# K and Q of head 0 in float32, ahead of the norm, for both halves of the sequence, with an opening in a fixed order

## The chip, the cores and the metric

The kernel runs on one core of a Trainium2 chip. The core has TensorE for matrix products (PE in the profile; PEld is its loading of weights), VectorE (DVE), ScalarE (ACT), GpSimd (POOL) and SyncE (SP, whose queue issues the DMAs here). The metric is the device time of one execution in microseconds (us); less is better.

## The reference

Two layers of a decoder with x of 1024 positions by 1024 channels, float32. What matters here is the start of layer 0: the norm, the projections, and the differential attention.

```python
u = rmsnorm(h, attn_norm[l])
proj = u @ w_in[l]
rq, rk, rv, rg, dq, dk, dv = jnp.split(proj, offsets, axis=-1)
...
dif = diff_attention(dq.reshape(B, S, DIFF_HEADS, 2, DIFF_HEAD_DIM),
                     dk.reshape(B, S, DIFF_HEADS, 2, DIFF_HEAD_DIM),
                     dv.reshape(B, S, DIFF_HEADS, DIFF_V_DIM), lam)
...
s = jnp.einsum('bqhjd,bkhjd->bhjqk', qb, kb).astype(jnp.float32) * scale
p = jax.nn.softmax(s, axis=-1)
a = p[:, :, 0] - lam * p[:, :, 1]
```

`rmsnorm` divides each position by the root of its mean square and multiplies by a gain per channel. Each of four heads has two score maps j of 64 channels, swept in blocks of 128 queries. Retention, the output projection, SwiGLU and layer 1 follow and are not touched.

## The kernel before

Everything is held with channels on the partitions and positions along the free dimension; the 1024 positions are two halves of 512 (`NH`, `HT`), the 1024 channels eight tiles (`KT`). Precision comes from splitting: a float32 value becomes a high part in float32r (a cast on ScalarE) and a low part, the remainder (a subtraction, on GpSimd for weights and on VectorE for u), and a product is three float32r matmuls, high by high, high by low and low by high (`mm3`, lines 288 to 290 in the profile; lines 323 to 325 are the same three in `tm_pair`, which makes the values V in pairs of position tiles, 256 columns each).

The opening of layer 0 runs in this order. x's half 0 and the weights of K and Q of head 0 are loaded in pieces. `fm_first` multiplies the unnormed x by weights into which the gains have been folded, in true float32 matmuls (line 307; one such matmul leaves two records in the trace), while the norm of half 0 is still being found: squares on ScalarE, their sums over channel tiles on VectorE (line 433), the sum over partitions by matmuls with ones (line 398), the root, and transposes that spread it over the partitions (line 414). `norm_half` then makes u in eight steps: a multiply (line 446), a cast (448) and a low part (450). K and Q of half 0 come by multiplying the product in PSUM by the root (line 696) and are put into stacks of high and low parts by `stack` (lines 522 and 523). Half 1 has the same norm, woven into the values of half 0; its K and Q are made from u with the split weights.

Then head 0's blocks: `att_block` makes the scores of both maps (lines 574 and 575), takes bias and maximum on VectorE (line 577), the exponential on ScalarE (581), scales and subtracts the maps (657, 666), and one block later `att_turn` transposes the result (line 600) for the product with V. `weave` puts other matmuls between: it takes from a fill so that the share of the fill that is done keeps up with that of the blocks. A unit of both is about one matmul of 512 columns. In head 0 the fill of blocks 0 to 3 is K, Q and V of half 1 (96 units), that of blocks 4 to 7 is K and Q of head 1 (96 units).

TensorE's order is the order in which the program is written, and each engine works off its own list in order. Outside `feed_forward`, the lists of the other engines and of SP's queue are set by a scheduler, which lets stacks and a few other operations go ahead (`high_priority`).

## Time and profile before

| | us |
|---|---|
| three runs: median (lowest to highest) | 2291.11 (2290.65 to 2291.35) |
| the profiled execution's own time | 2289.39 |
| its span, from the first to the last instruction | 2287.6 |
| TensorE busy in it | 2251.1 (98%) |
| VectorE busy | 1404.7 (61%) |
| ScalarE busy | 1009.1 (44%) |
| GpSimd busy | 731.7 (32%) |

The span is read against TensorE's busy time first: the difference is the time in which TensorE has nothing to do. "Busy" for a matmul includes its way through the array, so in a dense stream the distance from one start to the next is the cost of one and not its duration. In a row, the brackets at the end give the idle time of the engine just before it and what ended that.

### The profile page before, as it was taken

The numbers are of one execution on the slowest core, as the hardware profiler recorded it, in microseconds if no ns is written. First come the engines' busy times: TensorE is split into PE (matmuls) and PEld (weight loads), VectorE is DVE, ScalarE is ACT, GpSimd is POOL, SyncE is SP. The second block draws the span as 40 slices with busy tenths as digits, with TensorE's granted clock in tenths as the row PEclk, the third lists the DMA queues.
The fourth block names the chain that finished last, engine by engine and source line by source line (L and its number), as shares of the span: only waits on it lengthen the run. The fifth ranks groups of instructions, "written<-read, shape, count | busy, mean of one in ns | idle before, by whom it ended". The sixth has DMA issues, their size and how long they took to land.

```text
span 2287.6 us, 30632 instructions
## 1 busy us (share of the span) xinstructions
PE 2251.1 (98%) x11328; PEld 1895.3 (83%) x11328; DVE 1404.7 (61%) x2596; ACT 1009.1 (44%) x1905; POOL 731.7 (32%) x588
## 2 busy tenths in 40 slices
PE   7999999999999999999999999999999999999998
PEld 5888898787888888888888888988878888888887
DVE  8777612989534333995567774059884434359856
ACT  5666523445333333543256665234453333344332
POOL 3111212120455555335121112211215445544350
PEclk9999999999999999999999999999999999999999
DMA  4212121112433333652232222112123232346422
GB/s 164 79 47 65 44 95 38 55 57 63 137 106 103 105 106 90 230 186 96 72 99 56 56 65 88 52 37 74 49 95 120 93 115 93 110 148 202 157 65 74
DMA packets 74215, 216.58 MB, mean 95 GB/s; under 512 B 8017, under 2 KB 10065, under 8 KB 74065
## 3 DMA queue, kind: packets, MB, share of 16 engines
q1 hardware_dynamic: 74064, 214.62, 29.1%
q8 instruction: 89, 1.46, 0.3%
q14 instruction: 62, 0.50, 0.1%
HBM read 162.16 MB, written 44.04 MB: 90 GB/s over the span
## 4 chain that ended last, share of the span: by engine, by line
PE 84%; DVE 11%; ACT 2%; issue 1%; DMA 1%; POOL 0%; SPq 0%; DVEq 0%; ACTq 0%; POOLq 0%
PE ps_mm L264 8%; PE ps_mm L265 8%; PE ps_mm L266 8%; PE ps_mm L289 7%; PE ps_mm L288 7%; PE ps_mm L290 7%; PE ps_s L265 4%; PE ps_s L264 4%; PE ps_s L266 4%; PE ps_mm L323 3%; PE ps_mm L324 3%; PE ps_mm L325 3%; PE ps_t L265 2%; PE ps_t L264 2%; PE ps_t L266 2%
## 5 line engine op out<-in xcount | busy, mean ns | idle before, releaser
L241 POOL TENSOR_TENSOR w<-wr,w 128x512 fp32r<-128x512 f32 x262 | 368.2, 1419 | 442.9 <-ACT w L240 425.6
L281 POOL TENSOR_TENSOR w<-wr,w 128x512 fp32r<-128x512 f32 x140 | 186.2, 1337 | 577.3 <-ACT w L280 520.7
L288 PE MATMUL ps_mm<-u,w 128*128 128x512 f32 (+1 forms) x735 | 296.1, 403 | 0.0
L289 PE MATMUL ps_mm<-u,w 128*128 128x512 f32 (+1 forms) x735 | 287.2, 391 | 2.4 <-DVE u L450 2.4
L290 PE MATMUL ps_mm<-u,w 128*128 128x512 f32 (+1 forms) x735 | 286.5, 390 | 0.0
L240 ACT CAST w<-wr 128x512 fp32r<-128x512 f32 x312 | 187.2, 619 | 136.5 <-DVE wr L911 77.5
L264 PE MATMUL ps_mm<-u,w 128*128 128x512 f32 x432 | 168.5, 390 | 0.0
L266 PE MATMUL ps_mm<-u,w 128*128 128x512 f32 x432 | 168.1, 389 | 0.0
L265 PE MATMUL ps_mm<-u,w 128*128 128x512 f32 x432 | 168.1, 389 | 0.0
L290 PEld LDWEIGHTS ps_mm<-u,w 128*128 128x128 f32 x735 | 138.1, 188 | 30.1
L289 PEld LDWEIGHTS ps_mm<-u,w 128*128 128x128 f32 x735 | 138.6, 189 | 26.0 <-DVE u L450 3.1
L288 PEld LDWEIGHTS ps_mm<-u,w 128*128 128x128 f32 x735 | 138.3, 188 | 23.7
L960 ACT COPY t<-ps_mm 128x512 f32<-128x512 f32 x76 | 44.7, 588 | 240.3 <-PE ps_mm L266 240.3
L280 ACT CAST w<-wr 128x512 fp32r<-128x512 f32 x140 | 85.7, 619 | 128.6 <-PE ps_t L289 39.6
L325 PE MATMUL ps_mm<-w,u 128*128 128x256 f32 x448 | 127.2, 284 | 0.8 <-DVE u L450 0.8
L323 PE MATMUL ps_mm<-w,u 128*128 128x256 f32 x448 | 128.0, 286 | 0.0
L324 PE MATMUL ps_mm<-w,u 128*128 128x256 f32 x448 | 126.9, 283 | 0.0
L241 POOL TENSOR_TENSOR w<-t,w 128x512 fp32r<-128x512 f32 x48 | 65.1, 1357 | 191.9 <-ACT w L240 191.9
L577 DVE CUSTOM_DVE_ANT_0 sp<-ps_s,wr 128x512 f32<-128x512 f32 (+2 forms) x192 | 102.9, 552 | 32.3 <-PE ps_s L575 31.3
L581 ACT ACTIVATE sp<-sp,m 128x256 f32<-128x256 f32 (+7 forms) x128 | 99.2, 775 | 50.2 <-DVE m L580 49.4
L869 DVE TENSOR_TENSOR a<-a,ps_mm 128x512 f32<-128x512 f32 (+1 forms) x148 | 98.6, 667 | 27.6 <-PE ps_mm L266 14.5
L909 DVE TENSOR_TENSOR t<-wr,wr 128x512 f32<-128x512 f32 x46 | 32.8, 712 | 119.2 <-DMA wr<-wts 118.5
(386 smaller groups left out, 5919.7 us busy)
## 6 DMA issues: line engine op xcount, KB each, us to landing
wr<-wts SPq DMA_DIRECT2D x190, 512.0 KB, 3.7
mx<-s_fast SPq DMA_DIRECT2D x56, 512.0 KB, 4.9
s_fast<-mx SPq DMA_DIRECT2D x48, 512.0 KB, 4.8
kb<-ka SPq DMA_DIRECT2D x64, 128.0 KB, 2.3
s_rest<-mx SPq DMA_DIRECT2D x12, 512.0 KB, 2.9
kb<-wts SPq DMA_DIRECT2D x12, 512.0 KB, 5.4
mx<-s_rest SPq DMA_DIRECT2D x12, 512.0 KB, 3.3
a<-xT SPq DMA_DIRECT2D x16, 256.0 KB, 5.4
```

The costliest lines, as they stand in the source:

```text
L240: nc.scalar.copy(h, src)
L241: (eng or nc.gpsimd).tensor_tensor(out=o, in0=src, in1=h.bitcast(F32), op=ALU.subtract)
L264: mm(ps, lhsT=wh[:, c], rhs=bh, start=first and i == 0, stop=False, skip_group_check=True)
L265: mm(ps, lhsT=wh[:, c], rhs=bl, start=False, stop=False, skip_group_check=True)
L266: mm(ps, lhsT=wl[:, c], rhs=bh, start=False, stop=i == 3, skip_group_check=True)
L281: nc.gpsimd.tensor_tensor(out=o, in0=raw[:, cols], in1=h.bitcast(F32), op=ALU.subtract)
L288: mm(out, lhsT=lh, rhs=rh, start=first, stop=False)
L289: mm(out, lhsT=lh, rhs=rl, start=False, stop=False)
L290: mm(out, lhsT=ll, rhs=rh, start=False, stop=last)
L323: mm(o, lhsT=uh, rhs=wh, start=k == 0, stop=False)
L324: mm(o, lhsT=uh, rhs=wl, start=False, stop=False)
L325: mm(o, lhsT=ul, rhs=wh, start=False, stop=k == KT - 1)
```

## The change

K and Q of head 0 are now made by `fm_first` for both halves: 16 more float32 matmuls on the unnormed x, in the order K and Q of half 0, K and Q of half 1; the last two products go to the PSUM tags "o" and "t". The 48 float32r matmuls for K and Q of half 1 go, and with them the splits of the two weights. The root of half 1 is kept beside that of half 0, and `out` multiplies each product by its root. All low parts of u are on VectorE; before, two of half 0's were on GpSimd.

The stage up to the end of the values of half 0 is written out by hand in `opening`, under `manual_schedule` for ScalarE, VectorE, GpSimd and SP too: on each engine the order is that of the text. The values' two weights are loaded among the pieces of x's half 1. Q's stacks lie in "mx" and no longer in "a4", since x is still needed in "a4".

Head 0's eight blocks have one fill, V of half 1 and then K and Q of head 1: 48 + 96 = 144 units over all of them.

```diff
     def fm_first(self, h, ws):
 
-        for w in ws:
-            ps = self.bank("mm")
+        for (hf, w), tag in zip([(hf, w) for hf in range(NH) for w in ws], ("mm", "mm", "o", "t")):
+            ps = self.bank(tag)
+            self.first_ps.append(ps)
             for k in range(KT):
-                self.nc.tensor.matmul(ps, lhsT=w[:, P * k:P * k + P], rhs=h[k][:, 0:HT], start=k == 0,
-                                      stop=k == KT - 1)
+                self.nc.tensor.matmul(ps, lhsT=w[:, P * k:P * k + P], rhs=h[k][:, HT * hf:HT * hf + HT],
+                                      start=k == 0, stop=k == KT - 1)
                 yield 4
-            self.first_ps.append(ps)
+
 
...
-            eng = nc.gpsimd if keep and k in (1, 4) else nc.vector
-            eng.tensor_tensor(out=lo[:, k], in0=f, in1=hi[:, k].bitcast(F32), op=ALU.subtract)
-        if keep:
-            self.first_y = self.big("sp")[:, 0:HT]
-            nc.scalar.copy(self.first_y, y)
+            nc.vector.tensor_tensor(out=lo[:, k], in0=f, in1=hi[:, k].bitcast(F32), op=ALU.subtract)
...
     def attention(self, l, us, w_first, norm1):
         wk, wq, wdv = w_first
         nc = self.nc
-        v, qk, outs = {}, self.qk_tiles(), []
+        v, qk, outs = (self.first_v, self.first_qk, []) if l == 0 else ({}, self.qk_tiles(), [])
         kq = lambda hf: self.chain(self.stacks(wk, us, (hf,), qk[1], 1.0), self.stacks(wq, us, (hf,), qk[0], 0.125))
-        first = [self.chain(kq(hf), self.values(wdv, us, hf, v)) for hf in range(NH)]
         if l == 0:
-            for ps, st, scale in zip(self.first_ps, (qk[1], qk[0]), (1.0, 0.125)):
-                f = self.tmp()
-                nc.vector.tensor_tensor(out=f, in0=ps, in1=self.first_y, op=ALU.mult)
-                self.stack(f, st, slice(0, HT), scale)
-            self.weave(norm1, 40, self.values(wdv, us, 0, v), 48)
             self.late_consts()
         else:
+            first = [self.chain(kq(hf), self.values(wdv, us, hf, v)) for hf in range(NH)]
             self.weave(norm1, 96, first[0], 96)
         self.prev, self.norms, self.outs = None, [], []
         for h in range(4):
...
             A = self.att_open(h, qk, v, o)
             nqk = self.qk_tiles() if h < 3 else None
             self.att_swap(A, 0)
-            if h:
+            early = l == 0 and h == 0
+            if h or early:
                 self.att_swap(A, 1)
-            if h == 0:
+            if early:
+                pass
+            elif h == 0:
                 self.weave(self.att_part(l, A, 0, 4), PART0, first[1], 96)
                 self.att_swap(A, 1)
             elif h == 2:
...
             else:
                 fill = self.qk_head(us, nqk)
-            if h % 2:
+            if early:
+                self.weave(self.att_part(l, A, 0, 8), PART0 + PART1, self.chain(self.values(wdv, us, 1, v), fill), 144)
+            elif h % 2:
                 self.weave(self.att_part(l, A, 0, 8), PART0 + PART1, fill, 96 if h == 1 else 192)
             else:
                 self.weave(self.att_part(l, A, 4, 8), PART1, fill, 96)
...
+    def opening(self, h, raws, fold, us):
+
+        nc = self.nc
+        v = nc.vector.tensor_tensor
+        early = self.fm_first(h, fold)
...
+        def folds(i, c):
+            cs = slice(512 * c, 512 * c + 512)
             g = self.gains[:, 4 * c:4 * c + 4].rearrange("p (k o) -> p k o", o=1).broadcast_to([P, 4, P])
...
+
+        def square(hf, k):
+            s = self.big("kb")[:, 0:HT] if k else self.t("acc", 2, [P, 512])
+            nc.scalar.activation(s, h[k][:, half[hf]], AF.Square)
+            if k:
+                sq[hf, k] = s
+            else:
+                acc[hf] = s
+
+        def add(hf, k):
+            v(out=acc[hf], in0=acc[hf], in1=sq[hf, k], op=ALU.add)
+
+        def sums(hf):
+            ps = self.bank("s")
+            for t in range(4):
+                nc.tensor.matmul(ps[:, t:t + 1], lhsT=acc[hf][:, P * t:P * t + P],
+                                 rhs=self.ones[:, 0:1].bitcast(F32), start=True, stop=True)
...
+            xy[hf] = x, y
+
+        def root(hf):
...
+            ys[hf] = ps
+            us[hf] = [self.t("u", 4, [P, KT, HT], R32) for _ in range(2)]
+
+        def norm(hf, k):
+            f[k] = self.tmp()
+            nc.vector.scalar_tensor_tensor(out=f[k], in0=h[k][:, half[hf]], scalar=self.gains[:, k:k + 1], in1=ys[hf],
+                                           op0=ALU.mult, op1=ALU.mult)
+            nc.scalar.copy(us[hf][0][:, k], f[k])
+
+        def low(hf, k):
+            v(out=us[hf][1][:, k], in0=f[k], in1=us[hf][0][:, k].bitcast(F32), op=ALU.subtract)
+
+        def keep(hf):
+            y = self.big("sp")[:, 0:HT]
+            nc.scalar.copy(y, ys[hf])
+            ys[hf] = y
+
+        def out(i, to):
+            v(out=to, in0=self.first_ps[i], in1=ys[i // 2], op=ALU.mult)
+            return to
+
+        def stacks(i, src):
+            self.stack(src, qk[1 - i % 2], half[i // 2], (1.0, 0.125)[i % 2])
+
         for c in range(2):
             load_w(0, c)
             load(0, range(4 * c, 4 * c + 4))
         for c in range(2):
             load_w(1, c)
         self.wi = 2
+        wdv = [self.raw()]
+        load(1, range(4))
+        wdv.append(self.raw())
+        load(1, range(4, 8))
+        folds(0, 0)
+        for k in range(KT):
+            square(0, k)
+            if k == 4:
+                folds(0, 1)
+            if k:
+                add(0, k)
+        some(8)
+        folds(1, 0)
+        folds(1, 1)
+        wdv[0] = self.weight(raw=wdv[0])
+        sums(0)
+        square(1, 0)
+        some(3)
+        root(0)
+        some(5)
+        square(1, 1)
+        add(1, 1)
+        norm(0, 0)
...
+        square(1, 3)
+        add(1, 3)
+        wdv[1] = self.weight(raw=wdv[1])
+        norm(0, 2)
+        low(0, 1)
...
+        square(1, 7)
+        add(1, 7)
+        some(8)
+        norm(0, 4)
+        low(0, 3)
+        keep(0)
+        norm(0, 5)
+        low(0, 4)
+        sums(1)
+        norm(0, 6)
+        low(0, 5)
+        some(3)
+        root(1)
+        for _ in early:
+            pass
+        norm(0, 7)
+        low(0, 6)
+        low(0, 7)
+        kf, qf = [out(i, self.t("acc", 2, [P, 512])) for i in range(2)]
+        stacks(0, kf)
+        values = self.values(wdv, us, 0, self.first_v)
+        for k in range(KT):
+            norm(1, k)
+            if k:
+                low(1, k - 1)
+            if k == 3:
+                keep(1)
+            for _ in range(2):
+                next(values, None)
+        low(1, 7)
+        stacks(1, qf)
+        self.drain(values)
+        for i in (2, 3):
+            stacks(i, out(i, self.tmp()))
+        return None, None, wdv
+
...
+        e = mybir.EngineType
+        with self.tc.manual_schedule(engines={e.Activation, e.DVE, e.Pool, e.SP}):
+            w_first = self.opening(h, raws, fold, us)
+        h = self.layer(0, h, us, w_first, None, lambda h: [self.norm_half(h, 0, 8, nus)])
```

On TensorE, the place after the matmuls for Q of half 0 (`ps_mm_193` before, `ps_mm_187` after; `a_14` and so on are the tiles of x, `sp_99` and `sp_100` the folded weights of K and Q). Before:

```order
L307 MATMUL ps_mm_193<-a_20_95,sp_100 128x512
L307 MATMUL ps_mm_193<-a_21_96,sp_100 128x512
L398 MATMUL ps_s_294<-c_ones,acc_168 128x1 x4
L323 MATMUL ps_mm_308<-w_261,u_201 128x256
L324 MATMUL ps_mm_308<-w_262,u_201 128x256
L325 MATMUL ps_mm_308<-w_261,u_202 128x256
```

After, at the second product of half 1 (`ps_t_283`, Q; `ps_o_250` is K):

```order
L308 MATMUL ps_o_250<-a_20_95,sp_99 128x512
L308 MATMUL ps_o_250<-a_21_96,sp_99 128x512
L1254 MATMUL ps_s_269<-c_ones,acc_185 128x1 x4
L308 MATMUL ps_t_283<-a_14_89,sp_100 128x512
L308 MATMUL ps_t_283<-a_15_90,sp_100 128x512
L308 MATMUL ps_t_283<-a_16_91,sp_100 128x512
L1270 MATMUL ps_s_290<-c_ident,ny_275 128x128 x4
L308 MATMUL ps_t_283<-a_17_92,sp_100 128x512
```

The sums of half 1's squares stood ahead of the first values matmul; now they stand between the two products of half 1, the spreading of the root lies inside the second, and the values come after both.

On VectorE, the list up to block 0's last multiply, that of line 666 (`sp_496` is block 0's map, `z_497` its sums, `sp_537` block 1's map, `ka_280` a stack of K). Before:

```order
L580 TENSOR_REDUCE m_511<-m_511 128x1
L656 TENSOR_TENSOR z_497<-z_497,c_nlam 128x1
L523 SCALAR_TENSOR_TENSOR ka_280<-ps_mm_477,ka_280 64x512
L577 ISA sp_537,m_539<-ps_s_540,wr_467 128x256
L577 ISA m_539 128x1
L582 RECIPROCAL z_497<-z_497 128x1
L580 TENSOR_REDUCE m_539<-m_539 128x1
L666 SCALAR_TENSOR_TENSOR sp_496<-sp_496,z_497 128x128
```

After, where block 0's map is `sp_529` (the multiply is now line 663; `t_96` and `t_97` are K and Q of half 1 times the root, `mx_103` a stack of Q):

```order
L1292 TENSOR_TENSOR t_96_457<-ps_o_250,sp_369 128x512
L574 ISA sp_529,m_531<-ps_s_532,wr_488 128x128
L574 ISA m_531 128x1
L577 TENSOR_REDUCE m_531<-m_531 128x1
L520 SCALAR_TENSOR_TENSOR ka_105<-t_96_457,ka_105 64x512
L520 SCALAR_TENSOR_TENSOR ka_106<-t_96_457,ka_106 64x512
L1292 TENSOR_TENSOR t_97_463<-ps_t_283,sp_369 128x512
L579 RECIPROCAL z_530<-z_530 128x1
L574 ISA sp_529,m_547<-ps_s_548,wr_488 128x128
L574 ISA m_547 128x1
L577 TENSOR_REDUCE m_547<-m_547 128x1
L520 SCALAR_TENSOR_TENSOR mx_103<-t_97_463,mx_103 64x512
```

and, behind Q's second stack, block 1's first reading and a low part of half 1's values, the end of that list up to the multiply:

```order
L574 ISA sp_574,m_595<-ps_s_596,wr_488 128x256
L574 ISA m_595 128x1
L223 SCALAR_TENSOR_TENSOR c_nlam<-c_ex 128x1 x2
L577 TENSOR_REDUCE m_595<-m_595 128x1
L653 TENSOR_TENSOR z_530<-z_530,c_nlam 128x1
L653 TENSOR_TENSOR z_575<-z_575,c_nlam 128x1
L579 RECIPROCAL z_575<-z_575 128x1
L663 SCALAR_TENSOR_TENSOR sp_529<-sp_529,z_530 128x128
```

Between the first reading of block 0's scores and its last multiply stood one stack of K of half 1 and one reading of block 1; now both K and Q of half 1 are multiplied and stacked there, a low part of half 1's values and both readings of block 1 come before it too.

## Rows read from the trace of the kernel before

**Rows 1.** The page's first part: busy us of each engine, share of the span and instructions.

```profile
PE 2251.1 (98%) x11328; PEld 1895.3 (83%) x11328; DVE 1404.7 (61%) x2596; ACT 1009.1 (44%) x1905; POOL 731.7 (32%) x588
```
**Rows 2.** Busy time by stage: from and to and length in us, then for TensorE, weight loads, VectorE, ScalarE and GpSimd the busy us and instructions, then the granted clock as a share of 2.4 GHz, the DMA engines' busy share, and GB/s.

```profile
0.00:10.00 10.00, 4.57 (x6) 2.04 (x7) 3.75 (x8) 5.38 (x8) 2.35 (x8) 1.00 0.72 239
10.00:20.00 10.00, 8.78 (x23) 4.01 (x22) 8.64 (x12) 5.83 (x13) 4.69 (x4) 0.83 1.05 397
20.00:30.00 10.00, 8.39 (x36) 4.80 (x34) 9.86 (x13) 7.24 (x13) 6.43 (x4) 1.00 0.29 96
30.00:40.00 10.00, 7.15 (x40) 6.68 (x41) 9.03 (x17) 4.63 (x10) 3.15 (x3) 0.66 0.54 151
40.00:50.00 10.00, 10.00 (x70) 9.31 (x69) 9.91 (x16) 6.37 (x12) 1.28 (x6) 1.00 0.10 28
```
**Rows 3.** TensorE's timeline in the opening and to the first scores of head 1: start and duration in us, engine, line, operation, tiles, form, count, and in brackets the idle time before.

```profile
5.43 7.42 PE L307 MATMUL ps_mm<-a,sp 128*128 128x512 f32 x12 [5.43 <-DMA a<-xT]
14.07 1.05 PE L398 MATMUL ps_s<-c_ones,acc 128*128 128x1 f32 x8 [1.22 <-DVE acc L433]
14.98 5.38 PE L307 MATMUL ps_mm<-a,sp 128*128 128x512 f32 x8
20.63 5.32 PE L307 MATMUL ps_mm<-a,sp 128*128 128x512 f32 x12
...
27.55 1.02 PE L398 MATMUL ps_s<-c_ones,acc 128*128 128x1 f32 x8 [1.60 <-DVE acc L433]
...
30.83 0.58 PE L325 MATMUL ps_mm<-w,u 128*128 128x256 f32 x1 [0.84 <-DVE u L450]
...
33.20 0.58 PE L325 MATMUL ps_mm<-mx,u 128*128 128x256 f32 x1 [1.36 <-POOL u L450]
...
38.34 0.62 PE L414 MATMUL ps_s<-c_ident,ny 128*128 128x128 f32 x4 [0.66 <-DVE ny L410]
38.72 0.36 PE L323 MATMUL ps_mm<-mx,u 128*128 128x256 f32 x1
...
45.99 0.40 PE L288 MATMUL ps_mm<-u,w 128*128 128x512 f32 x1
...
50.10 0.28 PE L574 MATMUL ps_s<-ka,a 128*128 128x256 f32 x1
...
51.65 0.50 PE L289 MATMUL ps_mm<-u,w 128*128 128x512 f32 x1 [0.91 <-DVE u L450]
...
58.42 0.27 PE L600 MATMUL ps_t<-c_ident,sp 128*128 128x128 f32 x1
...
110.30 0.28 PE L574 MATMUL ps_s<-ka,a 128*128 128x256 f32 x1
```
**Rows 4.** Busy time by stages of 1 us, with the columns of the second group.

```profile
16.00:17.00 1.00, 1.00 (x3) 0.44 (x2) 1.00 (x1) 0.00 (x0) 1.00 (x2) 0.68 1.05 387
17.00:18.00 1.00, 1.00 (x2) 0.34 (x1) 0.49 (x3) 0.50 (x3) 0.28 (x1) 0.50 1.10 422
19.00:20.00 1.00, 1.00 (x3) 0.39 (x2) 0.85 (x2) 0.64 (x2) 0.00 (x0) 0.62 0.99 396
...
22.00:23.00 1.00, 1.00 (x4) 0.49 (x3) 1.00 (x3) 0.97 (x3) 0.00 (x0) 1.00 0.19 74
...
30.00:31.00 1.00, 0.17 (x1) 0.17 (x2) 1.00 (x2) 0.40 (x1) 1.00 (x2) 0.50 0.73 287
...
36.00:37.00 1.00, 1.00 (x7) 1.00 (x7) 0.94 (x4) 0.95 (x3) 0.00 (x0) 0.58 0.00 0
```
**Rows 5.** VectorE's timeline up to block 0's last multiply.

```profile
13.93 3.44 DVE L1232 TENSOR_TENSOR sp<-wr,c_gains 128x512 f32<-128x512 f32 x2
...
23.96 1.76 DVE L433 TENSOR_TENSOR acc<-acc,kb 128x512 f32<-128x512 f32 x1
...
27.98 1.10 DVE L450 TENSOR_TENSOR u<-t,u 128x512 fp32r<-128x512 f32 x1
...
32.68 2.22 DVE L450 TENSOR_TENSOR u<-t,u 128x512 fp32r<-128x512 f32 x3
...
42.53 1.90 DVE L450 TENSOR_TENSOR u<-t,u 128x512 fp32r<-128x512 f32 x3
...
56.38 0.42 DVE L577 CUSTOM_DVE_ANT_0 sp<-ps_s,wr 128x256 f32<-128x256 f32 x1
...
56.93 0.35 DVE L666 SCALAR_TENSOR_TENSOR sp<-sp,z 128x128 f32<-128x128 f32 x1
```
**Rows 6.** Groups of VectorE's instructions between 13.93 and 57.28 us: busy us and mean ns of one, and idle us ahead of them.

```profile
L547 DVE TENSOR_TENSOR v<-ps_mm,v 128x512 fp32r<-128x512 f32 x2 | 1.4, 680 | 0.0
L696 DVE TENSOR_TENSOR t<-ps_mm,sp 128x512 f32<-128x512 f32 x2 | 1.3, 678 | 0.0
```
**Rows 7.** GpSimd's timeline: a split of a weight, two low parts in one row.

```profile
25.14 3.40 POOL L281 TENSOR_TENSOR w<-wr,w 128x512 fp32r<-128x512 f32 x2
```
**Rows 8.** Busy time of longer stretches, with the columns of the second group: VectorE's list up to block 0's last multiply, from there to head 1's first scores, and head 1.

```profile
13.93:57.28 43.35, 37.84 (x189) 29.00 (x190) 40.75 (x76) 25.48 (x52) 16.95 (x18) 0.88 0.40 126
57.28:111.50 54.22, 54.22 (x324) 48.01 (x323) 38.95 (x112) 35.77 (x71) 11.13 (x12) 1.00 0.28 73
...
110.30:160.00 49.70, 47.76 (x279) 40.30 (x278) 42.43 (x129) 36.57 (x77) 6.57 (x12) 1.00 0.21 54
```
**Rows 9.** The end of the span, with the same columns.

```profile
2280.00:2284.00 4.00, 0.69 (x2) 0.29 (x2) 3.22 (x9) 0.00 (x0) 0.00 (x0) 0.50 0.39 128
```

More of the change, by code (lines that the diff above doesn't have):

```diff
@@ L1 @@
 import math
-from contextlib import ExitStack, nullcontext
+from contextlib import ExitStack
 import numpy as np
@@ L416, in rsqrt_rows, with squares @@
         return out[:, :cols]
-    def squares(self, h, sl, alone, kb=False, first=False):
+    def squares(self, h, sl, alone, kb=False):
         nc = self.nc
@@ L424, in squares @@
             s = (tmp() if k else self.t("acc", 2, [P, 512]))[:, :n]
-            with nullcontext() if first else self.tc.high_priority():
+            with self.tc.high_priority():
                 nc.scalar.activation(s, h[k][:, sl], AF.Square)
@@ L434, in squares, with norm_half @@
         return parts
-    def norm_half(self, h, hf, gcol, us, lag=11, gap=9, first=False, keep=False):
+    def norm_half(self, h, hf, gcol, us, lag=11, gap=9):
         nc = self.nc
         sl = slice(hf * HT, hf * HT + HT)
-        parts = self.squares(h, sl, 0, True, first)
+        parts = self.squares(h, sl, 0, True)
         yield lag
@@ L1220, in run @@
         fold = [self.big("sp") for _ in range(2)]
-        def load(hf, ks):
-            sl = slice(hf * HT, hf * HT + HT)
-            for k in ks:
-                nc.sync.dma_start(h[k][:, sl], self.a["xT"][k][:, sl])
-        def load_w(i, c):
-            cs = slice(512 * c, 512 * c + 512)
-            nc.sync.dma_start(raws[i][:, cs], self.a["wts"][i][:, cs])
-            g = self.gains[:, 4 * c:4 * c + 4].rearrange("p (k o) -> p k o", o=1).broadcast_to([P, 4, P])
-            v = lambda t: t[:, cs].rearrange("p (k m) -> p k m", m=P)
-            nc.vector.tensor_tensor(out=v(fold[i]), in0=v(raws[i]), in1=g, op=ALU.mult)
-        def some(n):
-            for _ in range(n):
-                next(early)
-        us, nus = {}, {}
-        for c in range(2):
-            load_w(0, c)
-            load(0, range(4 * c, 4 * c + 4))
-        for c in range(2):
-            load_w(1, c)
-        self.wi = 2
-        self.first_ps = []
-        early = self.fm_first(h, fold)
-        norm0 = self.norm_half(h, 0, 0, us, keep=True, gap=14)
-        norm1 = self.norm_half(h, 1, 0, us, 8, 14, True)
-        next(norm0)
-        some(6)
-        next(norm0)
-        load(1, range(KT))
-        next(norm1)
-        some(4)
-        self.drain(norm0, early)
-        wk, wq = [self.weight(raw=r) for r in raws]
-        wdv = [self.weight(), self.weight("mx")]
-        w_first = (wk, wq, wdv)
-        h = self.layer(0, h, us, w_first, norm1, lambda h: [self.norm_half(h, 0, 8, nus)])
+        us, nus = {}, {}
+        e = mybir.EngineType
+        with self.tc.manual_schedule(engines={e.Activation, e.DVE, e.Pool, e.SP}):
+            w_first = self.opening(h, raws, fold, us)
+        h = self.layer(0, h, us, w_first, None, lambda h: [self.norm_half(h, 0, 8, nus)])
         h = self.layer(1, h, nus, self.first_weights(), self.norm_half(h, 1, 8, nus, 34),
```

48 lines of the change are left out of this document (added).

## The prediction

> **What bounds the kernel now.** The page's first part comes first: TensorE is busy 2251.1 us of the span [rows 1], so only its idle or slow time can be won. The stages of 10 us show where that is [rows 2]: between 0 and 40 us TensorE is busy 4.57, 8.78, 8.39 and 7.15 of 10 us, and its granted clock falls to 0.83 and 0.66; from 40 it is near full. VectorE is at 8.64 to 9.91 of 10 us from 10 to 50.
>
> The timeline of TensorE gives the gaps [rows 3]: 1.22 and 1.60 us before the two sums of squares, 0.84 and 1.36 for low parts of u, 0.66 for the second norm, 0.91 at 51.65. The stages of 1 us show the clock at 0.50, that is 1.2 GHz in place of 2.4, for 3.4 us from 16.4 (0.68, 0.50 twice, 0.62) and for 6.8 from 30 (0.50 up to 0.58 in the seventh) [rows 4]. Four float32 matmuls (8 records from 14.98) take 5.38 us there; six (12 records from 20.63) take 5.32 at full clock: 0.887 us each.
>
> The place on which my argument turns I call **the mark**: the first transpose of head 0's block 0, at 58.42 [rows 3]. Before it TensorE waits on nothing but VectorE's list.
>
> **The change part by part.**
> TensorE's work: 48 matmuls of 512 columns go. 18 of that kind run from 45.99 to 50.10 [rows 3], 0.228 us each, so 10.9 us go. 16 float32 matmuls come at 0.887: 14.2. Net 3.3 us more work, but it needs only x, so it stands where TensorE waited.
>
> TensorE alone up to the mark: the sixth K matmul ends at 12.85 (5.43 + 7.42), two more 14.6; the sums of squares hold it 0.91 (14.07 to 14.98), 15.5; eight for Q 7.1 and the transposes 0.38 (38.34 to 38.72), 23.0; eight for K of half 1, 30.1; sums, 31.0; Q of half 1 with transposes, 38.5, and 0.7 for VectorE's root, as the 0.66 before; 39.2. The 96 matmuls of the values: 60 run from 38.72 to 45.99, 0.121 each, 11.6, so 50.8. Then 24 + 36 of half 1's values (7.3) and four pairs of scores of the same width (8 x 0.12): **59.1**.
>
> What is left behind the mark is smaller than before: there 3 matmuls for Q of half 1 and all 96 of its values stood behind it, now 36 values; 3 x 0.228 + 60 x 0.121 = 7.9 us less. So the mark may come as late as 58.42 + 7.9 = 66.3 at no loss. TensorE alone would win 66.3 - 59.1 = 7.2.
>
> VectorE up to the mark: before, from the folds of Q's weight at 13.93 [rows 5] to the end of block 0's last multiply (56.93 + 0.35 = 57.28) it works nearly without a break, 40.75 busy of 43.35 [rows 8]. ScalarE's casts that go stand ahead of that; the chain of squares is paced by VectorE's additions, so I leave 13.93. What comes in ahead of block 0's last multiply: two low parts that GpSimd did (2 x 0.63, from 1.90 for three [rows 5]), two multiplies of PSUM by the norm (2 x 0.68), two more halves of stacks (2 x 0.68 by the nearest rows), one low part of half 1's values (0.68) and one more reading of scores (0.42, as at 56.38): 5.1; 0.68 is the mean of the groups of these multiplies and low parts [rows 6]. That gives 62.4. Some 0.6 for new waits in the list (it reads the second pair of values, which TensorE ends at 50.8, only after ScalarE's copy): the mark at **63.0**. So VectorE decides, TensorE stands still 3.9 us ahead of the mark, and of the 7.2 us there remain 66.3 - 63.0 = 3.3.
>
> This 63.0 has two bounds. GpSimd's splits make VectorE's two-operand work slower: while GpSimd made four splits (two in 3.40 from 25.14 [rows 7], two more behind them) and a low part before, an addition took 1.76 at 23.96, three operations 1.09 to 1.11 (that at 27.98 is one), and three low parts 2.22 at 32.68 in place of 1.90 [rows 5]; over 0.63 each that is 2.8 us more. After the change four splits (two of a values weight, two of head 1's) fall into the same additions and low parts, so I keep 2.8. None of it gives 60.2, where TensorE nearly decides; each split in full, 4 x 1.70 = 6.8 us in place of 2.8, gives 67.0. I take the middle, since the row is of the same operations.
> The Trainium skill, "SBUF — State Buffer", section "Who interferes with whom", says that a VectorE instruction with two SBUF inputs contends with GpSimd's reads through one shared port, held by one engine for its whole instruction. The trace agrees that these suffer and that the low parts at 27.98 and 32.68 differ with what GpSimd does beside them; the loss of 2.8 against 6.8 us of splits says that the list rarely stands for a full split. By the rule in full the result would be 4 us worse than by the row.
>
> The clock behind the wait: the idle of 1.22 us at 12.85 was followed by 3.4 us at 0.50, the pieces from 25.95 to 33.20 went with 6.8 us, the 0.91 at 51.65 by none [rows 3, 4]. For the 3.9 us ahead of the mark I bound the loss at 0 and at half of 6.8, 3.4, and take half of 3.4: 1.7.
> The Trainium skill, "TensorE: Matmul & The Clock Gate", section "What's actually happening", has the array at half rate after idleness until it has been busy again; the rows at 0.50 bear it out, and this speaks against the change.
>
> One fill for eight blocks: head 0's blocks had 192 units of fill, now 144. Head 1, with 96, shows what thin fill costs: TensorE busy 47.76 of 49.70 [rows 8], 1.94 idle, with VectorE at 42.43. Head 0 behind the mark now needs TensorE for 110.30 - 58.42 - 7.9 = 44 us and VectorE for some 36 (38.95 before, less about 3 moved ahead of the mark), 82%. Bounds 0 (as head 0 before) and 3.9 (twice head 1); by head 1's rate over the 33 us of blocks 4 to 7, 1.3.
>
> Loads: SP's queue now has two values weights ahead of parts of x's half 1, 1 MB, with bias, tables and head 1's weights behind. DMA ran at 387 to 422 GB/s from 16 to 20 us, and by 22 us all that was queued had landed, 74 GB/s being left [rows 4]; 1 MB at 400 GB/s puts x back by 2.6 us within that time, and TensorE wants it from 23 on. I cost it at nothing.
>
> Sum: 3.3 - 1.7 - 1.3 = 0.3 won. The profiled run took 2289.39 us (span 2287.6 and 1.8 around it), 1.7 below the median; against the median, 2291.11 - 0.3 = **2290.8**. Behind head 0 the instructions stand in the order of before and TensorE bounds them, so the shift reaches the end.
>
> **The rivals.** (a) TensorE alone: VectorE's list is shorter than I count, the mark comes at 60 or before, no long wait, no clock loss: 66.3 - 59.1 - 1.3 = 5.9, 2285.2. For it: GpSimd has two splits and two low parts fewer in the opening, and an order set by hand may fit VectorE better than the scheduler's. Against: VectorE's share of 8.6 to 9.9 in rows 2.
> (b) Slower, by the clock: TensorE's wait ahead of the mark and the thin fill behind it leave it at 1.2 GHz for two stretches as long as that from 30 to 36 us; each costs half its 6.8 us. 3.3 - 6.8 - 1.3 = -4.8, 2295.9. It decides once over 13 us after the mark are at 0.50. For it: the clock at 0.50 at the very end too, where TensorE is busy 0.69 of 4 us [rows 9]. Against: head 1's 1.94 us of idle left it at 1.00 [rows 8].
> (c) GpSimd's splits in full: mark at 67.0, 4 us worse than the sum: 2294.8.
> (d) The change does not do what it says: x's half 1 lands late, and K of half 1 waits. It then loses its lead one for one; 3 us late gives 2293.5.
>
> **How the numbers follow.** The forecast has 0.61, (a) 0.17, (b) 0.13, (c) 0.06, (d) 0.03. The measurement tells about 0.2%, 4.6 us, from no change: 2286.5 to 2295.7. Faster: most of (a) and the forecast's lower edge, 0.22. Slower: most of (b), some of (c), 0.13. Same: 0.65. The range takes in (a) at 2285.2 and (b) at 2295.9: 2285 to 2296; the forecast's own bounds are 2287.5 to 2294.
>
> **What would show it.** Float32 matmuls without a gap over 1 us from 5.4 to about 39 us, at full clock; the first values matmul near 39, the first scores near 54; then a wait of 3 to 5 us for VectorE at the first transpose of block 0, near 63, with some us at 0.50 behind it; TensorE at head 1's first score some 0 to 3 us before 110.30. If that wait is missing, (a) holds and I have counted VectorE's list too long; if the 0.50 lasts past 70 us or comes back, (b). A wait of K of half 1 for x is (d). If the shift at head 1's first score is not the shift at the end, something behind head 0 moved, and the sum is wrong as a whole.

## The result and the profile after

The changed kernel takes 2295.09 us in the median of 21 runs; the kernel before, run beside it, 2290.41. One of the 21 runs took 8027.23 us and is left out of the ratio; the others lie between 2293.14 and 2298.16. The ratio is 1.0020, 95% interval 1.0014 to 1.0027: slower by 4.7 us, where 2290.8 was forecast. Its profiled execution has a span of 2292.8 us, 5.2 more than before.

The stages that answer to [rows 2], of the changed kernel, with the columns given there:

```profile
10.00:20.00 10.00, 10.00 (x32) 4.97 (x31) 6.67 (x13) 4.80 (x11) 2.49 (x2) 1.00 1.05 398
20.00:30.00 10.00, 10.00 (x24) 4.18 (x22) 8.14 (x10) 5.34 (x11) 4.49 (x3) 1.00 0.53 189
30.00:40.00 10.00, 7.36 (x23) 3.77 (x23) 8.98 (x17) 5.47 (x11) 1.54 (x1) 0.83 0.19 56
...
60.00:70.00 10.00, 6.27 (x39) 6.07 (x38) 6.01 (x27) 4.59 (x13) 0.00 (x0) 0.76 0.25 66
```

From 10 to 30 us TensorE now never stands still, as meant. VectorE, at 8.64 and 9.86 before, is at 6.67 and 8.14: it waits more, though it has more to do up to the mark. What was won there is lost in two holes, at 30 and at 60. TensorE's timeline shows them (it answers to [rows 3]):

```profile
23.08 7.03 PE L308 MATMUL ps_o<-a,sp 128*128 128x512 f32 x16
32.75 1.02 PE L1254 MATMUL ps_s<-c_ones,acc 128*128 128x1 f32 x8 [2.64 <-DVE acc L1249]
33.63 4.52 PE L308 MATMUL ps_t<-a,sp 128*128 128x512 f32 x6
...
42.32 0.68 PE L324 MATMUL ps_mm<-w,u 128*128 128x256 f32 x1
...
57.10 0.28 PE L571 MATMUL ps_s<-ka,mx 128*128 128x256 f32 x1
...
66.27 0.48 PE L597 MATMUL ps_t<-c_ident,sp 128*128 128x128 f32 x1 [3.73 <-DVE sp L663]
...
114.86 0.28 PE L571 MATMUL ps_s<-ka,a 128*128 128x256 f32 x1
```

K of half 1 ends at 30.1, as forecast; the sums of squares of half 1 come 2.64 us late, and the mark (the first transpose of block 0) is at 66.27 where 63.0 was forecast, after a wait of 3.73 us. Behind both waits the clock is at 1.2 GHz; the six records from 33.63 take 4.52 us there. The stretches below, of the same columns, are the half clock behind the mark, from the mark to head 1's first score, the end of that without the half clock, and VectorE's list from the folds of Q's weight to the mark:

```profile
66.27:72.05 5.78, 5.78 (x25) 5.78 (x26) 1.64 (x6) 1.22 (x3) 0.26 (x1) 0.50 0.00 0
66.27:114.86 48.59, 47.65 (x248) 40.72 (x249) 33.68 (x99) 31.73 (x63) 10.26 (x11) 0.94 0.24 64
72.05:114.86 42.81, 41.87 (x225) 34.94 (x224) 32.04 (x94) 30.51 (x61) 10.00 (x11) 1.00 0.28 73
13.12:66.27 53.15, 46.78 (x242) 32.47 (x240) 44.37 (x89) 28.68 (x58) 10.27 (x13) 0.96 0.38 122
```

With these the shift of head 1's first score, 110.30 to 114.86, can be put together term by term. TensorE needs 5.78 us at half clock for what I take as 2.9 us of work at full clock; 47.65 - 2.9 = 44.75 us of work at full clock lie behind the mark, where before all 51.88 us from 58.42 to 110.30 were busy [rows 3].

| term, us | forecast | measured |
|---|---|---|
| the mark, against 58.42 | +4.6 | +7.85 |
| less work of TensorE behind it | -7.9 | -7.1 |
| half clock behind the wait | +1.7 | +2.9 |
| idle in head 0's blocks (48.59 - 47.65) | +1.3 | +0.9 |
| head 1's first score | -0.3 | +4.55 |

The rest of the 5.2, 0.6 us, comes behind head 1's first score.

Why the mark is late stands in VectorE's row: of 53.15 us it is busy 44.37 and idle 8.78. Forecast were 49.1 us with 45.85 busy and 3.2 idle. Of the idle time 5.6 us lie ahead of 34 us (15.28 busy of 20.88 from 13.12 to 34). Here is how it idles there, first on VectorE (the first row, the folds, is read further below), then on ScalarE:

```profile
13.12 1.29 DVE L1238 TENSOR_TENSOR sp<-wr,c_gains 128x512 f32<-128x512 f32 x2
...
18.98 0.75 DVE L1279 SCALAR_TENSOR_TENSOR t<-a,c_gains,ps_s 128x512 f32<-128x512 f32 x1 [0.71 <-PE ps_s L1270]
20.95 0.69 DVE L1249 TENSOR_TENSOR acc<-acc,kb 128x512 f32<-128x512 f32 x1 [1.22 <-ACT kb L1242]
21.56 0.74 DVE L1279 SCALAR_TENSOR_TENSOR t<-a,c_gains,ps_s 128x512 f32<-128x512 f32 x1
22.21 0.68 DVE L1284 TENSOR_TENSOR u<-t,u 128x512 fp32r<-128x512 f32 x1
23.51 0.69 DVE L1249 TENSOR_TENSOR acc<-acc,kb 128x512 f32<-128x512 f32 x1 [0.61 <-ACT kb L1242]
```

```profile
19.77 0.62 ACT L1281 CAST u<-t 128x512 fp32r<-128x512 f32 x1 [2.23 <-DVE t L1279]
20.29 0.62 ACT L1242 ACTIVATE kb<-a 128x512 f32<-128x512 f32 x1
22.33 0.62 ACT L1281 CAST u<-t 128x512 fp32r<-128x512 f32 x1 [1.42 <-DVE t L1279]
22.86 0.62 ACT L1242 ACTIVATE kb<-a 128x512 f32<-128x512 f32 x1
```

The two lists wait for each other in turn. ScalarE stands 2.23 us for VectorE's multiply before it casts, and the square of half 1, which needs only x, is written behind that cast; VectorE's next instruction is the addition of that square and waits 1.22 us for it, with a low part and a multiply behind it that could run. The last piece is at the end of the list. The load of the lambda numbers stands on SP's queue behind the four copies of K of half 0 and two of the four of half 1 (the six in the first row), and the multiply that ends block 0 (L663) behind what is computed from them. SP's queue, then VectorE:

```profile
40.91 18.66 SPq L557 DMA_DIRECT2D kb<-ka  x6
59.62 0.58 SPq L211 DMA_DIRECT2D t<-lams  x1
```

```profile
62.48 0.16 DVE L579 RECIPROCAL z<-z 128x1 f32<-128x1 f32 x1
...
62.89 0.42 DVE L215 TENSOR_TENSOR t<-t 128x256 f32<-128x256 f32 x1
...
64.82 0.22 DVE L653 TENSOR_TENSOR z<-z,c_nlam 128x1 f32<-128x1 f32 x2
...
65.86 0.89 DVE L663 SCALAR_TENSOR_TENSOR sp<-sp,z 128x128 f32<-128x128 f32 x2
```

Block 0's sums are there at 62.48 (before, the lambda numbers were loaded at 47.03 and their result was written at 55.03, ahead of the first of block 0's sums at 55.18; here it is written at 64.61).

### The profile page after: what moved, and what is told of

Its sections match the earlier page's. It is cut to its first block, busy times and chain, and to the rows that moved or that the text cites. A ratio compares the mean times of both kernels' runs of the same rounds, so it can differ in the third digit from the quotient of the medians.

```text
span 2292.8 us, 30588 instructions
## 1 busy us (share of the span) xinstructions
PE 2256.2 (98%) x11312; PEld 1892.6 (83%) x11312; DVE 1398.9 (61%) x2600; ACT 1006.9 (44%) x1902; POOL 719.7 (31%) x582
## 4 chain that ended last, share of the span: by engine, by line
PE 80%; DVE 13%; ACT 3%; DMA 2%; issue 2%; POOL 0%; DVEq 0%; SPq 0%; ACTq 0%; POOLq 0%
PE ps_mm L264 7%; PE ps_mm L266 7%; PE ps_mm L265 7%; PE ps_mm L288 6%; PE ps_mm L289 6%; PE ps_mm L290 6%; PE ps_s L266 4%; PE ps_s L264 4%; PE ps_s L265 4%; PE ps_mm L324 2%; PE ps_mm L325 2%; PE ps_mm L326 2%; PE ps_t L266 2%; PE ps_t L264 2%; PE ps_t L265 2%
## 5 line engine op out<-in xcount | busy, mean ns | idle before, releaser
L288 PE MATMUL ps_mm<-u,w 128*128 128x512 f32 x719 | 289.8, 403 | 0.0
L289 PE MATMUL ps_mm<-u,w 128*128 128x512 f32 x719 | 280.9, 391 | 1.3 <-DVE u L450 1.3
L290 PE MATMUL ps_mm<-u,w 128*128 128x512 f32 x719 | 280.3, 390 | 0.0
L264 PE MATMUL ps_mm<-u,w 128*128 128x512 f32 x432 | 168.5, 390 | 0.0
L265 PE MATMUL ps_mm<-u,w 128*128 128x512 f32 x432 | 168.1, 389 | 0.0
L266 PE MATMUL ps_mm<-u,w 128*128 128x512 f32 x432 | 168.1, 389 | 0.0
L290 PEld LDWEIGHTS ps_mm<-u,w 128*128 128x128 f32 x719 | 135.1, 188 | 29.6
L289 PEld LDWEIGHTS ps_mm<-u,w 128*128 128x128 f32 x719 | 135.5, 189 | 24.0 <-DVE u L450 1.7
L288 PEld LDWEIGHTS ps_mm<-u,w 128*128 128x128 f32 x719 | 135.3, 188 | 23.1
L324 PE MATMUL ps_mm<-w,u 128*128 128x256 f32 x480 | 138.2, 288 | 0.0
L325 PE MATMUL ps_mm<-w,u 128*128 128x256 f32 x480 | 136.6, 285 | 0.0
L326 PE MATMUL ps_mm<-w,u 128*128 128x256 f32 x480 | 136.5, 284 | 0.0
```

Source lines behind the costliest of these rows:

```text
L264: mm(ps, lhsT=wh[:, c], rhs=bh, start=first and i == 0, stop=False, skip_group_check=True)
L265: mm(ps, lhsT=wh[:, c], rhs=bl, start=False, stop=False, skip_group_check=True)
L266: mm(ps, lhsT=wl[:, c], rhs=bh, start=False, stop=i == 3, skip_group_check=True)
L288: mm(out, lhsT=lh, rhs=rh, start=first, stop=False)
L289: mm(out, lhsT=lh, rhs=rl, start=False, stop=False)
L290: mm(out, lhsT=ll, rhs=rh, start=False, stop=last)
```

## The experiments

Three theories: (1) VectorE's list up to the mark ends late because it idles, by the order in which the opening is written; half clock follows the wait. (2) What is won ahead of the mark is lost behind it, by the thin fill. (3) GpSimd's splits hold VectorE. Medians are of 11 runs, the kernel before beside them at 2290.05 to 2290.52.

**The lambda numbers early.**

```diff
+        self.first_lv = self.tmp()
+        nc.sync.dma_start(self.first_lv, self.a["lams"])
         wdv = [self.raw()]
...
+        self.late_consts()
         wdv[0] = self.weight(raw=wdv[0])
```

> The changed kernel with the lambda numbers loaded behind Q's weight and computed behind the folds, so that block 0's final multiply no longer stands behind them. Theory 1 (VectorE's list ends late because it stands idle 8.8 us between 13.12 and 66.75, where 3.2 was counted; the lambda chain of load, dots, exponential is the last part of that): block 0's last multiply comes some 2.2 us earlier, the first transpose at about 64.0 in place of 66.27, TensorE's wait ahead of it about 1.5 us in place of 3.73, the time 2 to 5 us lower than the changed kernel's (2290 to 2293). Theory 2 (what is won ahead of the first transpose is given back behind it, by thin fill): first transpose earlier, head 1's first score still within 1 us of 114.9, time 2294 to 2296. Theory 3 (GpSimd's splits hold VectorE, nothing else): first transpose within 0.7 us of 66.27.

2292.10 us (2290.65 to 2294.39). Theory 1 half right. From the first scores to the mark it is 6.38 us (60.11 to 66.49) where it was 9.17 (57.10 to 66.27), so the lambda numbers did cost 2.8; TensorE waits 0.94 there and keeps its clock. But the mark did not move, since at the early place the same operations hold up the root of half 0 (ready at 19.50, before at 17.59), the half clock behind the late sums lasts 6.8 us in place of 3.4, and the first scores come 3 us later. Not all of that is the order: 0.85 us of it stands already at the folds (13.97 for 13.12), ahead of these operations, and the execution that was profiled is the slowest of the eleven (2294.39). Head 1's first score is at 112.86, 2.0 earlier.

**Half 1's squares early.**

```diff
         square(1, 0)
+        square(1, 1)
+        square(1, 2)
         some(3)
         root(0)
         some(5)
-        square(1, 1)
         add(1, 1)
+        square(1, 3)
         norm(0, 0)
-        square(1, 2)
         add(1, 2)
+        square(1, 4)
+        add(1, 3)
...
```

> The changed kernel with half 1's squares on ScalarE, and their additions on VectorE, moved ahead of the casts and low parts of half 0 they stood between, three squares at the start and then two to a round. Theory 1 (VectorE idles in the opening since these squares stand behind casts that wait for VectorE): VectorE's idle of some 5 us from 13 to 33 falls to about 2, the second sums of squares come within 0.5 us of K's last matmul (at 30.1; before 2.6 us later), no half clock from 34 to 38, the last low part of half 0 at 36 in place of 39.6, the first transpose at 62.5 to 63.5, the time 3.5 to 6.5 us lower (2288.5 to 2291.5). Theory 3 (GpSimd's splits make the additions and low parts slow): the idle turns into longer additions, the first transpose less than 1.5 us earlier, time 2293.5 to 2295.

2291.83 us (2290.50 to 2294.14). The time lies between what the two theories gave; the mark, at 64.94, is 1.3 earlier, which was theory 3's range, but the longer additions that theory 3 asked for are not there (the one stretched pair takes 2.55 us, 3.16 in the changed kernel). The sums are no longer late, but now TensorE waits for the root, which VectorE's list has behind two multiplies and low parts of half 0:

```profile
29.27 0.95 PE L1254 MATMUL ps_s<-c_ones,acc 128*128 128x1 f32 x8
30.08 2.82 PE L308 MATMUL ps_t<-a,sp 128*128 128x512 f32 x6
35.09 0.62 PE L1270 MATMUL ps_s<-c_ident,ny 128*128 128x128 f32 x4 [2.19 <-DVE ny L1267]
```

**Two fills.** Values of half 1 over blocks 0 to 3, K and Q of head 1 over 4 to 7, once on the changed kernel and once on the one with three changes of order, below.

```diff
-                self.weave(self.att_part(l, A, 0, 8), PART0 + PART1, self.chain(self.values(wdv, us, 1, v), fill), 144)
+                self.weave(self.att_part(l, A, 0, 4), PART0, self.values(wdv, us, 1, v), 48)
+                self.weave(self.att_part(l, A, 4, 8), PART1, fill, 96)
```

> The changed kernel with two fills for head 0's blocks again (half 1's values over blocks 0 to 3, K and Q of head 1 over 4 to 7), the total of 144 units as it is. Theory 1 (the loss is the late first transpose and the half clock behind it; idle behind them in head 0 is 0.9 us): time within 1 us of the changed kernel's (2294 to 2296). Theory 2 (the even fill over eight blocks is what costs): TensorE's idle between 80 and 110 goes, head 1's first score 1 to 2 us earlier, time 2293 to 2294.

2294.32 us (2293.81 to 2296.50), 0.8 below the changed kernel. TensorE's idle behind the mark goes (48.74 busy of 48.76 us), yet head 1's first score is only 0.7 earlier.

> The kernel with the three changes of order, and two fills for head 0's blocks in place of one. TensorE's idle between the first transpose and head 1's first score is 1.37 us there with one fill; if the even fill makes it, it falls to 0.5 or less, head 1's first score 0.7 to 1.4 us before 107.51, time 0.5 to 1.4 us lower. If VectorE's list makes it: within 0.5 us.

2289.77 us (2285.95 to 2291.42), against 2288.06 with one fill. Idle falls from 1.37 to 0.44 as written, but head 1's first score is at 107.84, where 0.7 to 1.4 before 107.51 was written, and the time is not lower: TensorE has 46.37 us of work in the stretch where it had 45.04. The idle was filled with work that would otherwise have stood behind; whether this costs or gains is within the spread. The fill is not where the 4.7 us are.

**Half 1's values in front of the mark**, and **work put into the wait.** The first moves 36 matmuls into TensorE's wait; the second adds 28 that nothing reads.

```diff
+                part, vals = self.att_part(l, A, 0, 8), self.values(wdv, us, 1, v)
+                lead = (next(part) for _ in range(8))
+                self.weave(lead, (PART0 + PART1) / 3, vals, 48)
+                self.weave(part, PART0 + PART1 - HEAD - sum(LAG) - sum(LAG[:3]) - 2, fill, 96)
```

> The changed kernel with all of half 1's values ahead of block 0's first transpose (36 matmuls that stood behind it go ahead, in TensorE's wait), the scores at their places, the rest of the fill over what is left. Theory 1 with the clock (the 3.7 us of waiting and the 2.9 us of half clock behind it are the loss): first transpose at about 66.9, no or a short wait, no half clock from 65 to 72, time 5 to 6.7 us lower (2288.4 to 2290). If only the wait counts and the clock drops all the same: 3 to 4 us lower (2291 to 2292). Theory 2 (fill taken from blocks 1 to 3 is missed there): time 2294 to 2297.

2290.76 us (2290.04 to 2293.72): 4.3 below the changed kernel, somewhat less than written. Mark at 67.59, no wait and no half clock there, head 1's first score at 109.62.

```diff
                         if n == 7:
+                            ps = self.bank("mm")
+                            for _ in range(28):
+                                nc.tensor.matmul(ps[:, 0:256], lhsT=us[0][0][:, 0, 0:P], rhs=wdv[0][0][0][:, 0:256],
+                                                 start=True, stop=True)
```

> The changed kernel, its order untouched, with 28 more matmuls of 256 columns (into a PSUM tile that nothing reads) between the last value matmul ahead of block 0's first transpose and that transpose, that is in TensorE's wait of 3.73 us; at 0.121 us each 3.4. They add work and move nothing else. If the half clock from 65.4 to 72.05 follows from TensorE standing still: first transpose within 0.5 us of 66.27, full clock behind it, head 1's first score 2.9 us earlier (about 112.0), time 2291.5 to 2293. If the half clock has another cause: head 1's first score within 0.5 us of 114.86, time 2294.5 to 2296.

2291.89 us (2290.58 to 2294.08), 3.2 faster than the changed kernel, with more work. TensorE's timeline, and the stretch from the mark to head 1's first score:

```profile
63.21 3.52 PE L725 MATMUL ps_mm<-w,u 128*128 128x256 f32 x28
67.01 0.33 PE L597 MATMUL ps_t<-c_ident,sp 128*128 128x128 f32 x1 [0.28 <-DVE sp L663]
```

```profile
67.01:113.27 46.26, 45.05 (x247) 38.13 (x248) 34.05 (x99) 31.84 (x63) 10.23 (x11) 1.00 0.25 67
```

All of this execution is 0.8 us later from the first scores on (57.93), so the mark is where it was against them; what changed is the clock, 1.00 throughout, and the stretch is 46.26 us in place of 48.59, with 45.05 busy in place of 47.65: 2.6 us by this, 2.9 by the halving above. Head 1's first score, at 113.27, is 1.6 earlier where 2.9 was written. The half clock behind this wait is the price of TensorE standing still, and theory 1's clock term is right; of the 3.2 us the stretch shows 2.3, and where the rest lies was not traced.

**Without the fixed order.** The opening's text stays, the scheduler orders ScalarE, VectorE, GpSimd and SP.

```diff
-        with self.tc.manual_schedule(engines={e.Activation, e.DVE, e.Pool, e.SP}):
+        if True:
             w_first = self.opening(h, raws, fold, us)
```

> The changed kernel without the fixed order: the opening's instructions on ScalarE, VectorE, GpSimd and SyncE are put in order by the scheduler, all else as it is. Theory 1 (the hand-set order of the opening leaves VectorE idle): VectorE's idle of 8.8 us ahead of the first transpose falls to 5 or less, first transpose 62 to 64, time 2289 to 2292. Rival (the order is no worse than the scheduler's; the work that the change puts ahead of the first transpose is what makes it late): first transpose at 66 or later, time 2294 to 2298.

2289.21 us (2287.54 to 2290.99): 5.9 below the changed kernel from this line alone, and 0.9995 (0.9986 to 1.0004) of the kernel before.

```profile
13.42:62.37 48.95, 45.70 (x239) 32.30 (x238) 44.79 (x84) 27.51 (x54) 11.23 (x13) 0.97 0.41 130
```

VectorE is as busy as under the fixed order (44.79 against 44.37) and idle 4.16 us in place of 8.78; the mark is at 62.37, without a wait of TensorE. Ahead of 34 us VectorE idles 1.5 us in place of 5.6. This shows the order as the cause of the late mark. It does so between the first scores and the mark (5.28 us in place of 9.17): the first scores come at 57.09, as under the fixed order, since TensorE here waits 3.09 us for the root of half 1, at 36.28.

**A fixed order with three changes.** Early squares as above; besides, the norm of half 1 right behind K's matmuls, and the lambda numbers loaded behind x and computed while half 1 is normalised.

```diff
         some(8)
         norm(0, 4)
         low(0, 3)
         keep(0)
+        sums(1)
         norm(0, 5)
         low(0, 4)
-        sums(1)
-        norm(0, 6)
-        low(0, 5)
         some(3)
         root(1)
...
                 keep(1)
+                self.late_consts()
```

> The changed kernel with three changes of order only: half 1's squares and additions early (two to a round), its norm right behind K's matmuls in VectorE's list, and the lambda numbers loaded behind x and computed while half 1 is normalised. Theory 1 (VectorE's idle decides): no TensorE wait over 0.7 us and no half clock between 15 and 60, first scores at about 53.5 (57.1 in the changed kernel), first transpose at 60 to 61.5, TensorE's wait there under 1.5 us; head 1's first score at 106 to 109 (114.86), time 2286.5 to 2289.5. Theory 2 (what is won ahead of the first transpose is given back behind it): head 1's first score at 111 or later, time 2291 to 2294. Theory 3 (GpSimd's splits): the additions and low parts lengthen, first transpose 63 or later.

2288.06 us (2286.82 to 2289.13), ratio 0.9990 (0.9981 to 0.9999). Its stretch from the folds to the mark, and TensorE there:

```profile
13.47:61.10 47.63, 44.64 (x240) 31.55 (x239) 43.88 (x83) 27.34 (x53) 10.63 (x13) 1.00 0.41 133
```

```profile
61.10 0.33 PE L594 MATMUL ps_t<-c_ident,sp 128*128 128x128 f32 x1 [0.90 <-DVE sp L660]
```

VectorE idles 3.75 us, the mark is at 61.10, the clock is full throughout, and head 1's first score is at 107.51. Missed by a little were the first scores (54.70 for 53.5) and the limit of 0.7 us on waits ahead of them (0.84 for the root, 1.1 there).

**On that kernel: values in front, and stacks deferred.** The values in front as above; the deferral takes half 1's four half stacks out of the list (`plain` leaves out their priority).

```diff
-        for i in (2, 3):
-            stacks(i, out(i, self.tmp()))
+        ends = [out(i, self.tmp()) for i in (2, 3)]
+        self.first_ends = lambda: [stacks(i, e, True) for i, e in zip((2, 3), ends)]
...
                         if n == 7:
+                            self.first_ends()
+                            self.att_swap(A, 1)
```

> The kernel with the early squares, norm and lambda numbers, and besides all of half 1's values ahead of block 0's first transpose. Theory 1: where the first transpose no longer waits, the values moved ahead only push it back by up to their 4.4 us, so it gains nothing over the kernel without them: time within 1.5 us of that one. If TensorE there still waits 3 us or more, 2 to 4 us lower than that one.

2291.69 us (2290.11 to 2292.63), 3.6 above the kernel without them, where 1.5 was the limit: a miss. TensorE idles 3.88 us behind the mark (41.09 busy of 44.97) against 1.37. Theory 2 would have it that fill taken from blocks 1 to 3 is missed there, but that is not the whole of it: the first try has the same fill and idles 1.61 behind its mark (40.42 busy of 42.03). The first wait has another cause in the trace, ScalarE's rows and then TensorE's:

```profile
70.69 0.62 ACT L277 CAST w<-wr 128x512 fp32r<-128x512 f32 x1 [2.58 <-DMA wr<-wts]
71.22 0.36 ACT L599 CAST a<-ps_t 128x256 fp32r<-128x256 f32 x1
```

```profile
71.64 0.39 PE L613 MATMUL ps_o<-a,v 128*128 128x256 f32 x1 [1.25 <-ACT a L599]
```

ScalarE's cast of a weight stands 2.58 us for its load, ahead of the cast that TensorE waits for and whose input TensorE had written by 68.6. It is the pattern of the opening again, now in the scheduler's list. What the moved fill itself costs stays open.

> As the kernel with early squares, norm and lambda numbers and half 1's values in front, and besides the four half stacks of half 1 (2.8 us of VectorE, 2.6 of ScalarE) taken out of the hand-set list and left to the scheduler behind the first transpose's values; it puts two of VectorE's four behind block 0's multiply. Theory 1: VectorE ends block 0 some 1.4 us earlier; worth up to 1.4 us where VectorE still decides the first transpose, nothing where TensorE does. Theory 2: nothing either way, or later (the keys of half 1 come later to block 4).

2287.79 us (2287.35 to 2289.74): with both, 3.9 below the values in front alone, where up to 1.4 was written, and not for the reason written: the mark is at 64.57 in both. The idle behind it falls from 3.88 to 1.63; ScalarE's wait for the weight is 1.33 us here and TensorE's behind it 0.51.

> The kernel with the three changes of order, and half 1's four half stacks left to the scheduler, which puts some of them behind block 0's multiply (VectorE two of four, 1.4 us). If VectorE still sets the first transpose there (0.9 us of waiting at 61.10): first transpose about 0.9 us earlier, time 0.5 to 1 us lower; if TensorE does: within 0.5 us.

2286.51 us (2285.23 to 2287.73), ratio 0.9983 (0.9974 to 0.9992): the best, 8.6 below the changed kernel and 3.5 below the one before. Written was 0.5 to 1 for the deferral; it is 1.5 (1.3 with each taken against the kernel before beside it), and not where it was expected: the mark (61.06) and head 1's first score (107.35) hardly move. In the profiled executions the two kernels are still 0.16 us apart at 1111 us (one matmul of line 285 starts at 1110.77 and 1110.93), and their spans 1.3 (2284.4 and 2285.7): the difference arises far behind the stacks that were deferred, so that the deferral makes it is not shown.

**GpSimd's splits.** The low parts of the values' weights on VectorE, on the kernel with three changes of order.

```diff
-            nc.gpsimd.tensor_tensor(out=o, in0=raw[:, cols], in1=h.bitcast(F32), op=ALU.subtract)
+            (eng or nc.gpsimd).tensor_tensor(out=o, in0=raw[:, cols], in1=h.bitcast(F32), op=ALU.subtract)
```

> The kernel with the three changes of order (early squares, norm, lambda numbers; 2288.06), and the four low parts of the values' weights made by VectorE in place of GpSimd. VectorE has 4 x 0.63 = 2.5 us more to do. If GpSimd's splits hold VectorE as much as its stretched operations of that kernel show (1.04 us in a small operation, 1.1 in an addition, 0.43 in a low part: 2.6 us), the first transpose stays within 0.7 us of 61.10 and the time within 1 us. If these stretches cost nothing further on: first transpose 2 to 2.5 us later, time 1.5 to 2.5 us higher.

2288.35 us (2286.31 to 2289.94), mark at 61.30: no change, with four splits of 0.6 us more in VectorE's list. From the folds to the mark it is busy 43.56 us, against 43.88 with the splits on GpSimd: it pays the same for them whoever makes them. The same operations of VectorE, first without GpSimd's split beside them (splits on VectorE), then with it (the kernel with three changes of order):

```profile
17.08 0.16 DVE L1261 TENSOR_TENSOR nx<-nx,ny 128x4 f32<-128x4 f32 x1
...
23.74 1.41 DVE L1244 TENSOR_TENSOR acc<-acc,kb 128x512 f32<-128x512 f32 x2
```

```profile
16.44 1.20 DVE L1261 TENSOR_TENSOR nx<-nx,ny 128x4 f32<-128x4 f32 x1
...
21.96 2.55 DVE L1244 TENSOR_TENSOR acc<-acc,kb 128x512 f32<-128x512 f32 x2
```

The operation of 128x4 ends, at 17.64, with the second of GpSimd's two splits (2.50 us for both from 15.12) and takes about as long as one of them, which agrees with the Trainium skill, "SBUF — State Buffer", section "Who interferes with whom": the shared port is held for a whole instruction. So theory 3's price is real, but it lies in the busy time, and that was below the forecast's (44.37 for 45.85); it does not explain why the mark was late.

## Why the prediction was wrong

**The step that failed** is "Some 0.6 for new waits in the list". The list of VectorE begins 0.8 us sooner than counted (13.12), is busy 1.5 less (44.37 for 45.85) and idle 5.6 more (8.78 for 3.2): 63.0 - 0.8 - 1.5 + 5.6 = 66.3, the measured mark. I took the idle of the scheduler's list, 2.6 us, over to a list in another order, and looked only at what each added instruction waits for, not at what is queued behind it on two engines at once. The runs put the extra idle down to order: the scheduler's order of the same work idles 4.16, a better one by hand 3.75. The busy time was lower since the folds of Q's weight, 3.44 us before [rows 5], took 1.29 (13.12 above): before, two of GpSimd's splits ran beside them (3.15 us from 13.67). The forecast counted a price of 2.8 us for the splits and missed that the folds held some 2.1 more of it.

**TensorE's walk** was right to 30.1 us, the end of K of half 1. There the sums were 2.64 late, and 3.4 us of half clock followed, so the values began at 42.32 in place of 39.2 and the first scores at 57.10 in place of some 54. At the mark this delay cost nothing: TensorE still had 3.73 us to wait there. One reading was wrong without bearing on the sum: ahead of the mark TensorE had waited not for VectorE's list alone, but once, 1.36 us, for a low part on GpSimd (33.20 [rows 3]).

**The work behind the mark** was taken 0.8 too large (7.9 for 7.1). **The clock** was taken as 1.7 and cost 2.9, within its bounds of 0 and 3.4, and the run with work in the wait confirms it as the wait's price. **The thin fill** cost 0.9 for 1.3. **The loads**: x came in time, as costed; what I overlooked on SP's queue was the load of the lambda numbers, 2.8 us of the list's end.

**The rivals.** (c) had the place and nearly the time, mark at 67.0 and 2294.8, but by luck: its cause, longer busy time by GpSimd's splits, was not there (44.37 us, less than the 45.85 counted). (b) had the sign and 2295.9; the half clock behind the mark lasted less than 6 us, not 13, so its condition was not met. (Its other sign, 0.50 past 70 us, was met on its face, to 72.05, since the mark came 3.3 us late.) What was said for (a), that an order by hand may fit VectorE better, was false for this order and true for the corrected one: its mark at 61.10 is near the 60 that (a) asked for, and it is 2.2 us below the kernel before beside it, where (a) gave 5.9.

**Of the signs** the wait of 3 to 5 us held (3.73) and the clock at 0.50 behind it; no gap over 1 us, the first values near 39, the first scores near 54, the mark near 63 and head 1's first score 0 to 3 us earlier did not. The last sign, that the shift at head 1's first score is the shift at the end, holds to 0.6 us for the changed kernel. It is not safe to read from one execution: that of the kernel with early lambda numbers gives back 2.4 us behind that point, 1.2 of it in one wait of TensorE for VectorE near 950 us, but it is the slowest of its eleven (2294.39, median 2292.10), so this may be the execution and not the kernel; that of the best kernel wins 0.3. Where the other parts lie was not traced.

## What to carry to other kernels

When two engines are given hand-written lists, walk them together: each instruction that waits for the other engine also holds what stands behind it, so work that needs nothing (here squares of x) belongs ahead of casts that wait, and the instructions that close a chain ahead of those that open the next. When a list is reordered, its idle time has to be worked out anew; its busy time can be carried over from the old trace only after a look at what ran beside it (the folds took 3.44 us beside GpSimd's splits and 1.29 without). A wait of TensorE on the path costs its length and, where the clock falls, more: an estimated 2.9 us behind the 3.73, and 1.7, half of 3.4, behind the 2.64. And single executions of one opening differ: the late sums stand at 32.34 to 33.61 in four kernels that share it, so a shift of a microsecond between two traces says little.

## What the runs showed of the hardware

A VectorE operation of 128x4 took 1.20 us beside GpSimd's split and 0.16 without it, so even so small an instruction can cost a microsecond there. The clock did not follow the length of a wait alone: 2.64 and 3.73 us in the changed kernel, and 2.19 with early squares, were followed by half clock, while 3.58 us ahead of that last kernel's mark were not. What decides is not shown. The stretch around that mark:

```profile
61.00:72.00 11.00, 7.42 (x57) 7.00 (x56) 7.17 (x31) 6.39 (x18) 2.54 (x2) 1.00 0.07 12
```
